# A two-layer hybrid backbone: the input gain of its linear recurrence, computed from tanh(x) and a squared decay, or from tanh(x/2) and the decay itself

## The chip, the cores and the metric

The kernel is one program on one core of a Trainium2 chip. The metric is device time in microseconds, the median of several runs. The profile and the trace come from one profiled execution. TensorE is called PE below, ScalarE is ACT, VectorE is DVE, GpSimd is POOL, and SP is the engine whose queue issues the DMAs.

## The reference, cut to what matters

The reference runs two layers over 1024 latent tokens and 256 context tokens. Each layer projects its input, runs three token mixers on the projections (global attention, windowed attention and a bidirectional gated linear recurrence), projects back, and runs a squared-ReLU MLP. The change touches the recurrence alone:

```python
def rglru_coeffs(x, w_a, b_a, w_i, b_i, lam):
    r = sigmoid(block_matmul(x, w_a) + b_a)
    i = sigmoid(block_matmul(x, w_i) + b_i)
    log_a = -LRU_C * r * softplus(-lam)
    u = sqrt(-expm1(2.0 * log_a)) * (i * x)
    return exp(log_a), u
...
h[n] = a[n] * h[n - 1] + u[n]
```

The recurrence is 512 channels wide and runs forwards and backwards over the context followed by the latent tokens. With x = log_a and a = exp(x), the factor in u is the root of 1 - a^2.

## The kernel before, in words

Features lie on the 128 partitions and tokens along the free axis. Tokens come in three tiles: two of 512 latent tokens (tile 0 and tile 1) and one of 256 context tokens (tile 2). The 512 channels of the recurrence are four chunks of 128. A product of two fp32 matrices is three matmuls on halves that are split into a high and a low part (lines 503 to 505, 685 to 687, 834 to 836 and others).

For each layer, Python generators write the work of several streams in turn: the convolution `conv_all`, the recurrence `lru_all`, the projections `side`, the attention `heads`, and in layer 0 the modulation. `weave` picks the stream that has the lowest sum of yielded costs so far, divided by a rate per stream. So the text order of the program hangs on the yielded costs alone. Within it, a scheduler decides at build time, by a simulated timeline (`schedule_with_timeline_sim=True`), in which order each engine gets its instructions. On the chip each engine then takes them in that order, one after the other.

`lru(c)` does the recurrence of one chunk c. `gates(d)` runs the gate matmuls of direction d into PSUM tiles named gate (a pool of four, shared with other work), then a Tanh for either gate, a DVE instruction for the input gate (line 693), and a third Tanh into the tile lt: t = tanh(x), since its scale and bias are both `nsp`, which is -4 softplus(-lam), and r is the tanh of half the gate's argument. `recur(d)` then runs two loops over the three token tiles:

- In the first loop ACT computes q = a^2 (the tile a2, printed as a) and a by two Exp instructions, and DVE computes (q + 1) * t at line 712, in place in lt.
- In the second loop ACT takes Ln of -t and Exp of half of that, both in place in lt. DVE multiplies u (the tile gate) by it at line 721, and runs the scan (line 724 forwards, line 729 backwards). The backward scan writes into q. Then the two directions are added (line 735) and multiplied by the gelu of the gate branch (line 736), and the result is stored by a DMA (line 737).

In the first chunks of a layer, while no attention job is prepared yet, the gates of both directions come first and the two `recur` are woven; `prog["prep"]` decides that.

Every activation goes through the helper `act` (line 131 in the profile), so the profile tells ACT's instructions apart by their tiles. Two table sets are used: Exp and Ln are in one, Tanh and Gelu in another. The helper puts a table load (line 127) where the set changes in the text order, and all instructions that need a set are kept between its load and the next one. Copies, squares and the like are in every set and may stand anywhere.

The tiles gate0, gate1, lt and a2, the tables tcos and tsin of the rotary embedding, q and k loads (qf, kf) and others share the pool `p` of 26 buffers of 128x512 fp32.

Of the kernel before, what the change touches and what calls it, by code (L numbers as in the profile page):

```python
# [11 lines left out]
AF = mybir.ActivationFunctionType  # L12
ALU = mybir.AluOpType
# [4 lines left out]
P = 128  # L18
# [3 lines left out]
DEPTH = 2  # L22
# [70 lines left out]
TOK = (512, 512, 256)  # L93
# [6 lines left out]
def tile_hybrid_backbone(ctx: ExitStack, tc: tile.TileContext, x, ctxt, cc, w_mod, b_mod, gains,  # L100
# [14 lines left out]
    vec = nc.vector  # L115
# [8 lines left out]
    def act(out, in_, func, **kw):  # L124
        want = tset.get(func)
        if want is not None and want != win["set"]:
            ld = nc.scalar.preload_act_table_set(want)
            for i in win["ins"]:
                tc.add_manual_dep(ld.ins, i.name, nosync, reason="table set")
            win.update(set=want, load=ld.ins, ins=[])  # L130
        r = nc.scalar.activation(out, in_, func, **kw)  # L131
        if want is not None:
            tc.add_manual_dep(r.ins, win["load"].name, nosync, reason="table set")
            win["ins"].append(r.ins)
        return r
# [15 lines left out]
    def weave(*pairs):  # L151
        live = [[g, rate, 0.0] for g, rate in pairs]
        while live:
            it = min(live, key=lambda v: v[2])
            try:
                cost = next(it[0])
            except StopIteration:
                live.remove(it)
                continue
            it[2] += cost / it[1]  # L160
            yield cost
# [14 lines left out]
    def utile(tt, dt=F32, name="ut"):  # L176
        if tt == CT:
            key = PAIRS.get(name, name)
            if key in halves:
                return halves.pop(key)  # L180
            t = upool.tile([P, 2, CTX], dt, tag="u", name=name + "c")
            halves[key] = t[:, 1, :]
            return t[:, 0, :]
        return upool.tile([P, 512], dt, tag="u", name=name)

    def ptile(n=512, dt=F32, name="pt"):
        return ppool.tile([P, 512], dt, tag="p", name=name)[:, 0:n]
# [7 lines left out]
    def sctile(n=512, name="sct"):  # L195
        return ps_sc.tile([P, n], F32, tag="sc", name=name)
# [4 lines left out]
    def cview(shape):  # L201
        n = int(np.prod(shape[1:]))
        v = cbuf[:, used[0]:used[0] + n]
        used[0] += n
        names = "abcde"[:len(shape) - 1]
        if len(names) > 1:
            v = v.rearrange("p (%s) -> p %s" % (" ".join(names), " ".join(names)),
                            **{m: d for m, d in zip(names, shape[1:])})
        return v
# [41 lines left out]
    c_eps, c_tiny, c_half = kc[:, 0:1], kc[:, 1:2], kc[:, 2:3]  # L251
# [13 lines left out]
    ab, th, e, z, z2, ser = (sp[:, i, :] for i in range(6))  # L265
# [19 lines left out]
    nsp = cview([P, DEPTH, 2, 4])  # L285
    vec.scalar_tensor_tensor(th, ser, 2.0, th, ALU.mult, ALU.add)
    vec.tensor_scalar(nsp.rearrange("p a b c -> p (a b c)"), th, -4.0, None, ALU.mult)
    nsp2 = cview([P, DEPTH, 2, 4])
    vec.tensor_scalar(nsp2.rearrange("p a b c -> p (a b c)"), th, -8.0, None, ALU.mult)

    def rstd_of(ps, n, bank=False, dst=None):
        l = ptile(n, name="rl")
# [294 lines left out]
    for l in range(DEPTH):  # L587
# [83 lines left out]
        def lru(c):  # L671
            dirs = ((2, 0, 1), (2, 1, 0))
            st1 = {}
            ghi, glo = gate_w[c]

            def gates(d):
                sc = nsp[:, l, d, c:c + 1]
                for tt in dirs[d]:
                    n = TOK[tt]
                    xh, xl = xs_split[c, tt]  # L680
                    res = []
                    for gi in range(2):
                        ps = sctile(n, "gate")
                        g = 2 * d + gi
                        mm(ps, ghi[:, g, :], xh, start=True, stop=False)
                        mm(ps, ghi[:, g, :], xl, start=False, stop=False)
                        mm(ps, glo[:, g, :], xh, start=False, stop=True)
                        s = ps if gi else ptile(n, name="gate0")
                        act(s, ps, AF.Tanh, scale=0.5, bias=lrubh[:, l, d, gi, c:c + 1])
                        res.append(s)  # L690
                    r, ig = res
                    i = ptile(n, name="gate1")
                    vec.scalar_tensor_tensor(i, ig, 1.0, XC[c, tt], ALU.add, ALU.mult)
                    t = ptile(n, name="lt")
                    act(t, r, AF.Tanh, scale=sc, bias=sc)
                    st1[d, tt] = (r, i, t)
                    if prog["prep"] == 0:
                        yield n / 256

            def gelus():  # L700
                for tt in outs:
                    act(GR[c, tt], GR[c, tt], AF.Gelu_apprx_tanh)

            def recur(d):
                sc, sc2 = nsp[:, l, d, c:c + 1], nsp2[:, l, d, c:c + 1]
                sq = {}
                for tt in dirs[d]:
                    a, u, t = st1[d, tt]
                    q = sq[tt] = ptile(TOK[tt], name="a2")
                    act(q, a, AF.Exp, scale=sc2, bias=sc2)  # L710
                    act(a, a, AF.Exp, scale=sc, bias=sc)
                    vec.scalar_tensor_tensor(t, q, 1.0, t, ALU.add, ALU.mult)
                    yield TOK[tt] / 400
                st = 0.0
                for tt in dirs[d]:
                    n = TOK[tt]
                    a, u, t = st1[d, tt]
                    q = sq[tt]
                    act(t, t, AF.Ln, scale=-1.0, bias=c_tiny)
                    act(t, t, AF.Exp, scale=0.5, bias=c_half)  # L720
                    vec.tensor_tensor(u, u, t, ALU.mult)
                    if d == 0:
                        h = utile(tt, name="hs")
                        vec.tensor_tensor_scan(h, a, u, st, ALU.mult, ALU.add)
                        st = h[:, n - 1:n]
                        HS[c, tt] = h
                    else:
                        h = q
                        vec.tensor_tensor_scan(h[:, ::-1], a[:, ::-1], u[:, ::-1], st, ALU.mult, ALU.add)
                        st = h[:, 0:1]  # L730
                        if tt in outs:
                            while (c, dirs[0][-1]) not in HS:
                                yield 0.5
                            hs = HS[c, tt]
                            ENG[HADD[l]].tensor_tensor(hs, hs, h, ALU.add)
                            ENG[HMUL[l]].tensor_tensor(hs, hs, GR[c, tt], ALU.mult)
                            nc.sync.dma_start(out=qd[f"f{4 + c}", tt], in_=hs)
                    yield n / 220

            pause = 1.5 if prog["prep"] == 0 else 5.0  # L740
            if cf["MERGE"] and prog["prep"] == 0:
                yield from gates(0)
                yield from gates(1)
                gelus()
                yield pause
                prog["conv"] = c + 1
                yield from weave((recur(0), 1), (recur(1), cf["MR"]))
            else:
                yield from gates(0)
                yield pause  # L750
                prog["conv"] = c + 1
                yield from recur(0)
                yield from gates(1)
                gelus()
                yield pause
                yield from recur(1)
# [629 lines left out]
```

## Time and profile before

| what | value |
| --- | --- |
| median of three runs | 3071.71 us (3069.28 to 3073.61) |
| the profiled execution | 3065.88 us |
| its span, first to last instruction | 3064.1 us |
| mean granted clock of TensorE | 0.975 |

The span is 1.8 us shorter than the profiled execution's own time, and that time is 5.8 us below the median. A granted clock of 1.00 is 2.4 GHz and one of 0.50 is 1.2 GHz; numbers between are means over a stretch. Times in the rows are in microseconds from the first instruction. The recurrence runs from about 120 to 305 us in layer 0 and from about 1790 to 1970 us in layer 1.

### The profile page before, as it was taken

Reading aid. Unit: us, or ns where it says so; the run is one execution under the profiler, and the core shown is the slowest. Engines: PE = TensorE matmul, PEld = TensorE weight load, DVE = VectorE, ACT = ScalarE, POOL = GpSimd, SP = SyncE. Lnnn points to the kernel's source line nnn. Section 1 sums busy time; section 2 is a strip of 40 time slices with the busy share of each in tenths; the row PEclk is TensorE's granted clock in tenths of the full one; section 3 lists DMA queues with packets and bytes.
Section 4 is the critical chain, followed back from the end, with each engine's and each line's share of the span. In section 5 each row is a group of like instructions: output and inputs, shape, how many; then the busy total and the mean of one; then the engine's idle time right before and its main releaser. Section 6 shows DMA issues by size and latency. Waiting matters only on the chain. (4 is left out here: it accounts for less than half of the span.)

```text
span 3064.1 us, 39201 instructions
## 1 busy us (share of the span) xinstructions
PE 2886.9 (94%) x14562; PEld 2213.2 (72%) x14562; DVE 1680.3 (55%) x2695; ACT 1225.7 (40%) x2284; POOL 1144.8 (37%) x883
## 2 busy tenths in 40 slices
PE   6997899999998999999999799699998999999997
PEld 4876645546877888888888688454466888888886
DVE  6776664556367243334736876785374562333465
ACT  4587343345343312112323578543354332112232
POOL 1453232333555322223434231343356543334232
PEclk9998999999999999999999899899998999999999
DMA  7222554434233111112213412320043321111142
GB/s 248 64 85 93 169 163 146 160 125 151 93 121 127 42 39 38 35 42 69 97 59 117 150 59 71 134 70 31 15 136 108 116 95 49 48 49 59 61 153 66
DMA packets 169424, 287.27 MB, mean 94 GB/s; under 512 B 23824, under 2 KB 37648, under 8 KB 169232
## 3 DMA queue, kind: packets, MB, share of 16 engines
q1 hardware_dynamic: 169232, 284.76, 28.5%
q8 instruction: 114, 1.87, 0.3%
q14 instruction: 78, 0.64, 0.1%
HBM read 249.56 MB, written 35.13 MB: 93 GB/s over the span
## 5 line engine op out<-in xcount | busy, mean ns | idle before, releaser
L481 POOL TENSOR_TENSOR wlo<-raw,whi 128x512 fp32r<-128x512 f32 x484 | 699.2, 1459 | 722.0 <-ACT whi L131 417.8
L1219 DVE TENSOR_TENSOR acc<-acc,m 128x512 f32<-128x512 f32 (+1 forms) x488 | 321.3, 675 | 319.7 <-PE m L1212 318.6
L1211 PE MATMUL m<-h1lo,whi 128*128 128x512 f32 (+1 forms) x1296 | 474.7, 367 | 4.4 <-DVE h1lo L1201 4.4
L1212 PE MATMUL m<-h1hi,wlo 128*128 128x512 f32 (+1 forms) x1296 | 472.3, 367 | 0.0
L131 ACT ACTIVATE whi<-raw 128x512 fp32r<-128x512 f32 x552 | 325.1, 621 | 353.7 <-PE m L1211 157.6
L1210 PE MATMUL m<-h1hi,whi 128*128 128x512 f32 (+1 forms) x1296 | 457.6, 367 | 3.1 <-ACT sq L131 1.5
L503 PE MATMUL m<-hhi,whi 128*128 128x512 f32 x1024 | 403.1, 394 | 5.2 <-ACT hhi L131 5.2
L504 PE MATMUL m<-hlo,whi 128*128 128x512 f32 x1024 | 400.4, 391 | 2.9 <-DVE hlo L519 2.9
L505 PE MATMUL m<-hhi,wlo 128*128 128x512 f32 x1024 | 399.6, 390 | 0.0
L1197 POOL TENSOR_TENSOR relu<-relu 128x512 f32<-128x512 f32 (+1 forms) x160 | 161.9, 1012 | 617.3 <-ACT relu L131 597.5
L1201 DVE TENSOR_TENSOR h1lo<-relu,h1hi 128x512 fp32r<-128x512 f32 (+1 forms) x160 | 142.7, 892 | 443.6 <-ACT h1hi L131 443.6
L131 ACT ACTIVATE relu<-m 128x512 f32<-128x512 f32 (+1 forms) x160 | 88.3, 552 | 581.5 <-PE m L505 571.8
L1211 PEld LDWEIGHTS m<-h1lo,whi 128*128 128x128 f32 x1296 | 244.6, 189 | 45.7 <-DVE h1lo L1201 5.2
L1210 PEld LDWEIGHTS m<-h1hi,whi 128*128 128x128 f32 x1296 | 242.7, 189 | 46.3 <-DVE acc L1219 2.1
L1212 PEld LDWEIGHTS m<-h1hi,wlo 128*128 128x128 f32 x1296 | 244.6, 189 | 41.3
L503 PEld LDWEIGHTS m<-hhi,whi 128*128 128x128 f32 x1024 | 193.6, 189 | 47.3 <-ACT hhi L131 6.8
L504 PEld LDWEIGHTS m<-hlo,whi 128*128 128x128 f32 x1024 | 193.1, 189 | 44.0 <-DVE hlo L519 3.6
L505 PEld LDWEIGHTS m<-hhi,wlo 128*128 128x128 f32 x1024 | 192.9, 188 | 40.8
L131 ACT ACTIVATE prob<-sc 128x512 f32<-128x512 f32 (+3 forms) x288 | 141.3, 530 | 201.9 <-PE sc L970 191.6
L995 POOL TENSOR_TENSOR prob<-prob 128x1024 f32<-128x1024 f32 (+2 forms) x62 | 134.5, 2170 | 227.2 <-ACT prob L131 138.7
L989 PE MATMUL pv<-prob,vt 128*64 128x512 f32 (+3 forms) x576 | 199.0, 552 | 2.3 <-ACT prob L131 1.6
L503 PE MATMUL zin<-hhi,whi 128*128 128x512 f32 x424 | 171.6, 405 | 1.9 <-DVE zsh L789 1.9
(344 smaller groups left out, 5289.6 us busy)
## 6 DMA issues: line engine op xcount, KB each, us to landing
raw<-in_w SPq DMA_DIRECT2D x392, 256.0 KB, 3.5
rawm<-in_w_mod SPq DMA_DIRECT2D x192, 256.0 KB, 4.2
raw<-in_w_in SPq DMA_DIRECT2D x88, 256.0 KB, 3.1
raw<-in_w_out SPq DMA_DIRECT2D x64, 256.0 KB, 4.0
xres<-xs SPq DMA_DIRECT2D x40, 256.0 KB, 5.1
xs<-y SPq DMA_DIRECT2D x32, 256.0 KB, 2.5
fc<-qf SPq DMA_DIRECT2D x30, 256.0 KB, 4.6
tcos<-in_cos SPq DMA_DIRECT2D x24, 256.0 KB, 3.3
```

The lines of the kernel that those rows point to most:

```text
L131: r = nc.scalar.activation(out, in_, func, **kw)
L481: (vec if on_dve(key) else gp).tensor_tensor(lo, raw, f(hi), ALU.subtract)
L503: mm(ps, wh, xh, start=(k == first), stop=False)
L504: mm(ps, wh, xl, start=False, stop=False)
L505: mm(ps, wl, xh, start=False, stop=(k == last))
L989: mm(pv[half[h], q0:q1], V[kt, j][:, vcol + 64 * h:vcol + 64 * h + HD], pt[:, h, :], start=(ui == 0), stop=(ui == len(units) - 1), skip_gr ...
L1197: gp.tensor_tensor(r, r, r, ALU.mult)
L1201: vec.tensor_tensor(lo, r, f(hi), ALU.subtract)
L1210: mm(ps, wh, h1[p][0][:, c0:c1], start=(p == 0), stop=False)
L1211: mm(ps, wh, h1[p][1][:, c0:c1], start=False, stop=False)
L1212: mm(ps, wl, h1[p][0][:, c0:c1], start=False, stop=(p == 1))
L1219: vec.tensor_tensor(a, a, ps, ALU.add)
```

## The change

With x = log_a, 1 - a^2 = -(1 + a^2) tanh(x), and also 1 - a^2 = -(1 + a)^2 tanh(x/2). The kernel before takes the root of the first form. The changed kernel takes (1 + a) times the root of -tanh(x/2). The scale and bias of the third Tanh are half as large. The Exp that made q is gone, and with it the tile a2. Ln and Exp of the root move from the second loop to the first, in front of the Exp that makes a. DVE still has two elementwise instructions for each tile: u times the root, now in the first loop, and (a + 1) times u, now in the second. The backward scan writes into t. The yields keep their places and costs.

```diff
-    nsp2 = cview([P, DEPTH, 2, 4])
-    vec.tensor_scalar(nsp2.rearrange("p a b c -> p (a b c)"), th, -8.0, None, ALU.mult)
+    nsph = cview([P, DEPTH, 2, 4])
+    vec.tensor_scalar(nsph.rearrange("p a b c -> p (a b c)"), th, -2.0, None, ALU.mult)
...
             def gates(d):
-                sc = nsp[:, l, d, c:c + 1]
+                sc = nsph[:, l, d, c:c + 1]
...
             def recur(d):
-                sc, sc2 = nsp[:, l, d, c:c + 1], nsp2[:, l, d, c:c + 1]
-                sq = {}
+                sc = nsp[:, l, d, c:c + 1]
                 for tt in dirs[d]:
                     a, u, t = st1[d, tt]
-                    q = sq[tt] = ptile(TOK[tt], name="a2")
-                    act(q, a, AF.Exp, scale=sc2, bias=sc2)
+                    act(t, t, AF.Ln, scale=-1.0, bias=c_tiny)
+                    act(t, t, AF.Exp, scale=0.5, bias=c_half)
                     act(a, a, AF.Exp, scale=sc, bias=sc)
-                    vec.scalar_tensor_tensor(t, q, 1.0, t, ALU.add, ALU.mult)
+                    vec.tensor_tensor(u, u, t, ALU.mult)
                     yield TOK[tt] / 400
                 st = 0.0
                 for tt in dirs[d]:
                     n = TOK[tt]
                     a, u, t = st1[d, tt]
-                    q = sq[tt]
-                    act(t, t, AF.Ln, scale=-1.0, bias=c_tiny)
-                    act(t, t, AF.Exp, scale=0.5, bias=c_half)
-                    vec.tensor_tensor(u, u, t, ALU.mult)
+                    vec.scalar_tensor_tensor(u, a, 1.0, u, ALU.add, ALU.mult)
...
-                        h = q
+                        h = t
```

## Rows read from the trace of the kernel before

**Rows 1.** The page: busy time, share of the span and instructions of each engine.

```profile
PE 2886.9 (94%) x14562; PEld 2213.2 (72%) x14562; DVE 1680.3 (55%) x2695; ACT 1225.7 (40%) x2284; POOL 1144.8 (37%) x883
```

**Rows 2.** Instructions on the tile a (ns min/median/max); engine idle until (us, times).

```profile
L131 ACT ACTIVATE a<-gate,cbuf x48: 587/803/819, 139.2 to 1949.8; 128x512 f32<-128x512 f32 x32, 128x256 f32<-128x256 f32 x16
L712 DVE SCALAR_TENSOR_TENSOR lt<-a,lt x48: 418/684/1780, 139.8 to 1953.7; 128x512 f32<-128x512 f32 x32, 128x256 f32<-128x256 f32 x16
...
  ACT a L131: 35.6, 24
```

**Rows 3.** The same view of the tile lt.

```profile
L131 ACT ACTIVATE lt<-lt,cbuf x96: 492/709/727, 141.9 to 1955.1; 128x512 f32<-128x512 f32 x64, 128x256 f32<-128x256 f32 x32
...
  ACT lt L131: 16.8, 14
```

**Rows 4.** Waits of PE from 100 to 340 us: total, times, longest.

```profile
PE gate L685 <- ACT gate L131: 8.4, 2, 7.1
PE mx L901 <- ACT qh L131: 7.4, 1, 7.4
PE mx L913 <- DVE zsh L789: 5.1, 1, 5.1
PE zin L503 <- DVE zsh L789: 1.9, 1, 1.9
```

**Rows 5.** Waits of PE from 1760 to 2070 us.

```profile
PE mx L901 <- ACT qh L131: 14.2, 1, 14.2
PE mx L913 <- DVE zsh L789: 4.2, 1, 4.2
PE vps L834 <- ACT gl L131: 3.6, 1, 3.6
PE zn L806 <- DVE cbuf L908: 3.5, 1, 3.5
```

**Rows 6.** Timeline of PE: the first matmul after the gap in layer 0.

```profile
250.34 0.79 PE L685 MATMUL gate<-xh,ghi 128*128 128x512 f32 x1 [7.07 <-ACT gate L131]
```

**Rows 7.** Timeline of ACT in the stretch before that gap ends.

```profile
235.13 0.59 ACT L131 ACTIVATE a<-gate,cbuf 128x256 f32<-128x256 f32 x1
235.62 0.49 ACT L131 ACTIVATE lt<-lt,cbuf 128x256 f32<-128x256 f32 x1
236.02 0.59 ACT L131 ACTIVATE gate<-gate,cbuf 128x256 f32<-128x256 f32 x1
...
241.39 0.80 ACT L131 ACTIVATE a<-gate,cbuf 128x512 f32<-128x512 f32 x1
242.10 1.32 ACT L131 ACTIVATE lt<-lt,cbuf 128x512 f32<-128x512 f32 x2
...
248.52 1.28 ACT L127 ACT_TABLE_LOAD   x1
```

**Rows 8.** Windows: stretch, its length, busy time by engine, granted clock, DMA share, GB/s.

```profile
233.00:250.00 17.00, 10.27 (x81) 9.66 (x79) 9.40 (x15) 16.89 (x27) 1.68 (x2) 0.90 0.00 1
250.30:253.50 3.20, 3.16 (x12) 2.87 (x13) 3.20 (x4) 3.20 (x9) 0.19 (x2) 0.51 0.12 41
...
1881.60:1885.00 3.40, 3.40 (x16) 3.40 (x17) 3.40 (x6) 2.56 (x5) 1.97 (x2) 0.50 0.23 74
...
1936.60:1976.00 39.40, 14.55 (x57) 9.51 (x55) 37.64 (x73) 20.72 (x36) 9.86 (x7) 0.71 0.30 104
```

**Rows 9.** Timeline of ACT at the end of layer 0's recurrence.

```profile
298.81 1.38 ACT L131 ACTIVATE kh<-kf 128x512 fp32r<-128x512 f32 x2 [1.82 <-DVE rl L296]
300.51 0.63 ACT L131 ACTIVATE qh<-qf 128x512 fp32r<-128x512 f32 x1 [0.32 <-DMA qf<-qb]
```

**Rows 10.** Timeline of ACT in layer 1, at two gaps of PE.

```profile
1876.38 0.63 ACT L131 ACTIVATE whi<-raw 128x512 fp32r<-128x512 f32 x1 [0.79 <-DVE a L729]
...
1880.94 0.60 ACT L131 ACTIVATE gl<-zin 128x512 f32<-128x512 f32 x1
...
1951.74 0.62 ACT L131 ACTIVATE qh<-qf 128x512 fp32r<-128x512 f32 x1
```

## The prediction

> **What bounds the kernel now.** I read the page first. PE is busy for 94% of the span and ACT for 40% [rows 1]. So an ACT instruction is worth something only where PE stands still for it, and I looked for those places. The tile view gives what the change removes; the waits of PE, asked for the stretches of the recurrence alone, give where PE stands. In layer 0 one wait of 7.1 us stands out: a gate matmul waits for an ACT gate instruction. After it come, at the end of the recurrence, 7.4 us for qh (ACT) and 5.1 us for zsh (DVE) [rows 4]. In layer 1 there is 3.6 us for gl (ACT), then 14.2 us for qh, 4.2 us for zsh and 3.5 us for a DVE reduction [rows 5]. Elsewhere in these stretches PE is fed.
>
> The gap of layer 0 is plainly ACT's. It ends at 250.34 [rows 6]. ACT was busy for 16.89 of the 17 us from 233 to 250, PE for 10.27 [rows 8], and the work is one chunk's `recur`, then a table load at 248.52 [rows 7]. The gate matmuls of the next chunk had filled their PSUM tiles, and the Tanh that empties them may only run behind that load. After the gap PE runs 3.2 us at a granted clock of 0.51 [rows 8], that is, at 1.2 GHz after having stood still.
>
> **The change, part by part.**
>
> *The removed Exp.* There are 48, 32 of 512 columns and 16 of 256 [rows 2]; two layers of four chunks make eight, so a chunk has four and two. ACT starts the next instruction a little before the one before it ends, so I price them by the distance of starts: 242.10 - 241.39 = 0.71 us for 512 columns, and 235.62 - 235.13 = 0.49 us for 256 [rows 7]. A chunk saves 4 x 0.71 + 2 x 0.49 = 3.8 us of ACT time, the kernel eight times that, 30 us. What counts is where PE waits for it:
>
> - The gap of layer 0 (7.07 us): all six stand in front of the Tanh, and ACT has no idle time into which the saving could go. It shrinks by 3.8 us, to 3.3. The clock may add to that: the 3.2 us at half speed did the work of 1.6. The 3.6 us gap of layer 1 was followed by 3.4 us at 0.50 as well [rows 8], so a gap of 3.3 us may still cost the clock. I take 0 and keep 1.6 as an end.
> - The end of layer 0: qh there starts 0.32 us after idle time that a DMA ended, and kh waited for DVE before it [rows 9]. ACT is not saturated; the chain runs through DVE, the store of a projection and its reload. It gets shorter only as far as DVE waited for ACT before. Ends are 0 and 3.8; I take 1, nearer to the end without gain, since the row names DMA.
> - The 3.6 us gap of layer 1: gl starts at 1880.94 behind a run of the recurrence. But ACT idled 0.79 us for DVE at 1876.38 [rows 10], so part of the saving would fall into that wait. Ends 0 and 3.6; I take 2, about the middle.
> - The end of layer 1: qh starts at 1951.74 [rows 10] and ends the 14.2 us wait; the six removed Exp of the last chunk all stand before it. But from 1936.6 to 1976 DVE is busy for 37.64 of 39.4 us [rows 8], and the later waits of PE there are for DVE. A qh 3.8 us earlier meets a full DVE queue, whose work stays. DVE's idle time, 39.4 - 37.64 = 1.8 us, is what can be gained without another order; I take 1.5, and 3.8 as the far end.
>
> *The moved Ln and Exp.* No instruction is added: 96 before and after [rows 3]. Moved in front of the Exp for a, they no longer wait for a DVE result that itself waited for ACT. That round trip cost DVE 35.6 us of idle time at line 712 [rows 2] and 16.8 us at line 721 [rows 3]. DVE is not the bound in most of these stretches, so I book nothing for it. The price is that the first DVE instruction of a tile now waits for Ln and Exp where it waited for one Exp: this is the second rival below. No DMA is moved, and no queue of SP or POOL is passed by anything but shorter waits.
>
> *The DVE instructions.* Two elementwise ones for each tile before and after, all operands in SBUF, so 0. Their spread is wide: line 712 takes 418 to 1780 ns, 684 in the median [rows 2], and the slow ones lie beside POOL work. Whether the moved ones land beside POOL more often I can't see; an extra 1.1 us each (1780 - 684) on DVE is the bound, against the same gained where they escape it. By the Trainium skill, page "SBUF — State Buffer", section "SBUF: two separate sides", DVE instructions with two SBUF inputs and GpSimd instructions that read SBUF exclude one another for a whole instruction. Taken alone that rule would allow any of the moved ones to turn slow, where the row's median says that most are not.
>
> *The tile a2.* It leaves the pool of 26 buffers, six at a time in the woven chunks. Less waiting for buffers can only start loads earlier; the PE waits above name other causes, so 0, with the gain inside the ends already given.
>
> *The set-up and table loads.* One constant instead of another, and the set changes in the text order at the same places: 0.
>
> The sum is 3.8 + 1 + 2 + 1.5 = 8.3 us. The profiled execution took 3065.88 us, so it would take 3057.6; its time lies 5.8 us below the median of the runs, and on that median I get 3071.7 - 8.3 = 3063.4 us, 0.27% less. About 0.2%, 6 us, is what a measurement of this kernel can tell from no change.
>
> The largest gain of all terms is 3.8 + 1.6 in the first gap, 3.8 at the end of layer 0, 3.6 + 1.7 (half of 3.4 us of slow clock) in the third, 3.8 at the last: 18.3 us. With a few microseconds for slow clock behind the two end gaps, about 3050 us.
>
> **The rivals.**
>
> *1. The gain is given back; no change.* PE's own work is untouched, 2886.9 us [rows 1]. The 3.8 us won at 250 us can be lost at 301 us if kh and qh come when the DMA brings them, and in layer 1 DVE sets the end at 1976 whatever ACT does. For it speak DVE's 37.64 of 39.4 us and the DMA in front of qh [rows 8, 9]. Against it speaks that what ends late there also started late: the last chunk's gates come after the gap, so that chain moves forward with it. Time: 3071.7 us, or 3067.9 if the first gap alone counts. The planner that orders the queues may also fill the free time of ACT with other work in front of the Tanh, so that the change does nothing there. By the Trainium skill, page "Perfetto Trace Analysis", section "Identifying Performance Opportunities", a kernel gets better mainly through its most-contended engine. That is PE here, and the rule would leave the time as it is; the same page also says to look at the gaps of that engine, and the 7.07 us gap is one that ACT ends [rows 6].
>
> *2. DVE waits longer in the first loop; slower.* In that loop a tile of 512 columns now takes ACT Ln, Exp and Exp, where it took two Exp. Ln or Exp on lt costs 1.32 - 0.71 = 0.61 us by the distance of starts, and 0.40 for 256 columns (236.02 - 235.62) [rows 7]. So the loop takes 2 x 0.61 - 0.71 = 0.51 us more for 512 columns and 2 x 0.40 - 0.49 = 0.31 for 256, and a chunk's last product comes 4 x 0.51 + 2 x 0.31 = 2.7 us later. DVE works in order: if zsh, kl and the reductions for the attention stand behind it, PE gets them 2.7 us later. PE waited for DVE in four places: zsh twice in layer 0 and zsh and the reduction in layer 1 [rows 4, 5]. Four times 2.7 is 10.8 us, less the 3.8 of the first gap: 7.0 slower, 3078.7 us. It decides only if at least three of the four are queued that way. Against it: the second loop then has no wait for ACT at all, so the same queue catches up within the chunk.
>
> **How the numbers follow.** The forecast, faster by more than 0.2%, gets 0.54: with 3.8 us from the first gap it needs 2.4 us more, and I book 4.5 in the other three places. Rival 1, within 0.2%, gets 0.29, and rival 2, slower by more than 0.2%, gets 0.17. The range from 3050 to 3077 us leaves about 0.05 out below and up to 0.15 above, the larger part of rival 2. The forecast's own range is 3050 to 3065.
>
> **What would show it.** Right: 48 fewer ACT instructions and some 34 us less ACT time (32 x 0.80 + 16 x 0.60); no Exp into the tile a; the wait of the gate matmul near 245 us down from 7.1 to about 3.3; the waits for gl and for qh in layer 1 each shorter by 1 to 4 us; DVE no longer idle for a tile a. Wrong: the first gap as long as it was, for instance because other ACT work moved in front of the Tanh; or the first gap shorter and the waits for qh, zsh and the reductions longer by as much; or longer DVE idle time for lt in the first loop with PE waiting behind it. If gaps move outside these two stretches, the order of the queues has changed, and my terms are not what decides.

## The result and the profile after

The changed kernel takes 3110.6 us (median, 3106.0 to 3123.7) against 3070.5 us for the kernel before in the same runs: a ratio of 1.0138, interval 1.0105 to 1.0172. It is 40 us slower; the prediction was 3063.4 us, with a range from 3050 to 3077.

The line of the page that answers to [rows 1], of the kernel after:

```profile
PE 2924.6 (94%) x14562; PEld 2236.6 (72%) x14562; DVE 1651.2 (53%) x2695; ACT 1209.2 (39%) x2236; POOL 1126.3 (36%) x883
```

ACT lost its 48 instructions and 16.5 us. PE ran the same 14562 matmuls and was busy for 37.7 us longer. The profiled spans are 3064.1 and 3104.1 us, so of 40.0 us more, 37.7 are PE's work and 2.3 its idle time.

Where these 37.7 us lie is seen in the view of stretches, one row for each stage: set-up with the recurrence of layer 0, its attention with the projection back, MLP and projections, recurrence of layer 1, its attention, its MLP. The columns are the stretch, its length, busy time (and instructions) of PE, PEld, DVE, ACT and POOL, granted clock, DMA share and GB/s. First the kernel before:

```profile
0.00:300.00 300.00, 251.76 (x1422) 208.50 (x1422) 204.13 (x359) 206.33 (x364) 106.82 (x88) 0.96 0.37 122
300.00:810.00 510.00, 480.36 (x2767) 287.51 (x2768) 285.09 (x518) 203.22 (x417) 186.68 (x144) 0.97 0.46 149
810.00:1780.00 970.00, 940.97 (x4869) 804.14 (x4868) 499.30 (x776) 303.55 (x578) 357.38 (x289) 0.99 0.24 77
1780.00:1935.00 155.00, 151.31 (x815) 131.27 (x814) 104.88 (x153) 129.66 (x224) 47.10 (x35) 0.99 0.23 76
1935.00:2390.00 455.00, 405.49 (x1780) 241.13 (x1779) 271.10 (x440) 195.38 (x362) 195.33 (x142) 0.94 0.24 78
2390.00:3064.10 674.10, 657.06 (x2917) 540.60 (x2915) 315.81 (x450) 187.53 (x341) 251.48 (x189) 0.99 0.24 78
```

The same view of the kernel after, with the stages cut where nearly the same work ends (see the counts of matmuls):

```profile
0.00:300.00 300.00, 248.44 (x1422) 206.93 (x1422) 199.77 (x358) 188.22 (x337) 110.59 (x89) 0.97 0.36 118
300.00:830.00 530.00, 497.93 (x2754) 296.55 (x2755) 281.76 (x518) 205.85 (x416) 176.84 (x141) 0.94 0.44 143
830.00:1800.00 970.00, 943.91 (x4875) 805.49 (x4874) 492.78 (x777) 308.92 (x578) 351.11 (x291) 0.99 0.24 78
1800.00:1960.00 160.00, 152.36 (x812) 130.90 (x811) 101.42 (x153) 117.14 (x205) 48.02 (x34) 0.98 0.22 72
1960.00:2430.00 470.00, 425.07 (x1782) 254.51 (x1781) 265.26 (x440) 194.59 (x358) 192.89 (x142) 0.93 0.23 76
2430.00:3104.00 674.00, 656.91 (x2926) 542.20 (x2924) 310.16 (x451) 194.47 (x344) 246.87 (x192) 0.99 0.24 79
```

The two attention stages got 20 and 15 us longer, and in them PE is busy for 17.6 and 19.6 us more with nearly the same matmuls (13 fewer and 2 more). The change touches not a line of the attention. The MLPs are within 3 us of what they were, and the recurrence of layer 1 is 5 us longer.

Which matmuls these are is told by the same view of one tile over the whole run (stretch, length, busy time of PE, PEld and the engine that reads the tile; the end at 3130 lies behind the span). The first row is the scores sc, the second the maxima mx; the kernel before:

```profile
0.00:3130.00 3130.00, 203.30 (x1152) 129.37 (x1152) 141.31 (x288) 0.97 0.28 92
0.00:3130.00 3130.00, 89.12 (x352) 44.60 (x352) 170.09 (x336) 0.97 0.28 92
```

The kernel after:

```profile
0.00:3130.00 3130.00, 225.17 (x1152) 144.47 (x1152) 143.97 (x288) 0.97 0.28 92
0.00:3130.00 3130.00, 101.88 (x352) 52.06 (x352) 171.73 (x336) 0.97 0.28 92
```

So the 1504 matmuls of sc and mx cover 34.6 us more of PE's time (21.9 and 12.8). They contract over 64 rows: head 0 in one half of the array, head 1 in the other. The timeline of PE shows what is different (start, duration, line, tiles, how many). In the kernel before, the two heads stand next to each other:

```profile
450.14 0.40 PE L970 MATMUL sc<-qh,kh 64*128 64x512 f32 x2
450.37 0.40 PE L970 MATMUL sc<-ql,kh 64*128 64x512 f32 x2
450.60 0.39 PE L970 MATMUL sc<-qh,kl 64*128 64x512 f32 x2
450.83 0.39 PE L970 MATMUL sc<-qm,neg_sb 64*128 64x512 f32 x2
451.06 0.39 PE L921 MATMUL mx<-kh,qh 64*128 64x512 f32 x1
```

In the kernel after there are places where one head stands alone:

```profile
457.58 0.40 PE L966 MATMUL sc<-qh,kh 64*128 64x512 f32 x1
457.59 0.50 PE L917 MATMUL mx<-kh,qh 64*128 64x512 f32 x1
457.82 0.39 PE L966 MATMUL sc<-ql,kh 64*128 64x512 f32 x1
458.06 0.39 PE L966 MATMUL sc<-qh,kl 64*128 64x512 f32 x1
458.29 0.39 PE L966 MATMUL sc<-qm,neg_sb 64*128 64x512 f32 x1
```

From 450.14 to 451.06 PE does eight matmuls of 512 columns, two at a time, each pair in 0.23 us. From 457.82 to 458.29 the steps are 0.23 and 0.24 us as well, but each holds one matmul. In these rows the second of a pair costs nothing, and alone it costs 0.23 us. The Trainium skill, page "TensorEngine Tiling (Array Packing)", section "Theoretical Speedup", gives up to 2x where the contraction is over 64 rows at most; these rows agree. Over the whole kernel a pair gains less: in the kernel before, a pair of sc with 512 columns covers 0.29 us on average and a single one 0.22, so a pair saves 0.15 us.

**How far the pairs go.** I went through PE's queue in the two programs and paired off neighbours of different halves, each matmul in one pair at most. In the kernel before 806 of the 1504 matmuls are in such pairs, in the kernel after 646. That is 80 pairs fewer, at up to 0.23 us each 18 us at most, and 12 at the average of 0.15. A second part is the clock. I summed PE's busy time over the stretches in which the trace has a granted clock of 0.50: 85.7 us before, 115.1 after. At 0.50 a matmul takes about twice as long (in the kernel after the gate matmuls of 512 columns start 0.43 us apart at 0.50, at 246.38 and 246.81 us, and 0.23 us apart at 1.00, at 260.87 and 261.10), so PE's busy time less half of that is its **work at full clock**: 2886.9 - 42.8 = 2844.1 us before, 2924.6 - 57.5 = 2867.1 after. So 23.0 of the 37.7 us are work in the same matmuls, and 14.7 come from work done at 1.2 GHz. All of the 23.0 lies in sc and mx: counted as the time by which their matmuls move PE's end on, and corrected for the clock in the same way, sc takes 177.7 us before and 189.8 after, mx 59.8 and 70.9. The lost pairs explain 12 to 18 us of it; where the rest comes from is not shown.

**Why the queue changed.** The planner of this kernel first lays the work out with the numbers of buffers that are written in the kernel. For the kernel before it finds no order that way, and raises five numbers by one. It says so when the program is built:

```
the starting buffer counts deadlocked; feasible after 1 bump round(s); {'p_p_64': '26→27',
'mm_ps_mm_76': '3→4', 'raw_raw_70': '6→7', 'hi_wsp_73': '6→7', 'sc_ps_sc_79': '4→5'}
```

For the kernel after, without a2 in the pool p, the written numbers do, and they stay: 3 for mm and 4 for sc, both PSUM. The scores take their tiles from sc. The maxima mx take head 0's from sc and head 1's from mm, which the projections use too. So the theory: **the change took away two PSUM buffers that nobody had written down, and with them the pairs.** The rivals: the recurrence itself (ACT's or DVE's new order) costs the time; or the order changed in other ways, and the pairs are only a part.

### The profile page after: what moved, and what is told of

It reads as the page before. It is cut to its first block, busy times and chain, and to the rows that moved or that the text cites. A ratio compares the mean times of both kernels' runs of the same rounds, so it can differ in the third digit from the quotient of the medians.

```text
span 3104.1 us, 39454 instructions
## 1 busy us (share of the span) xinstructions
PE 2924.6 (94%) x14562; PEld 2236.6 (72%) x14562; DVE 1651.2 (53%) x2695; ACT 1209.2 (39%) x2236; POOL 1126.3 (36%) x883
## 4 chain that ended last, share of the span: by engine, by line
PE 77%; DVE 9%; ACT 3%; issue 3%; DMA 2%; POOL 1%; SPq 0%; POOLq 0%; DVEq 0%; ACTq 0%
PE m L504 8%; PE m L503 8%; PE m L505 8%; PE m L1206 8%; PE m L1207 8%; PE m L1208 8%; PE sc L966 6%; PE pv L985 5%; PE yps L503 2%; PE yps L504 2%; PE yps L505 2%; PE zin L503 2%; PE zin L504 2%; DVE sq L322 2%; PE zin L505 2%
## 5 line engine op out<-in xcount | busy, mean ns | idle before, releaser
L481 POOL TENSOR_TENSOR wlo<-raw,whi 128x512 fp32r<-128x512 f32 x484 | 671.9, 1402 | 1118.3 <-ACT whi L131 946.6
L131 ACT ACTIVATE whi<-raw 128x512 fp32r<-128x512 f32 x552 | 333.4, 626 | 716.0 <-PE m L1207 363.3
L1197 DVE TENSOR_TENSOR h1lo<-relu,h1hi 128x512 fp32r<-128x512 f32 (+1 forms) x160 | 118.0, 737 | 345.0 <-ACT h1hi L131 344.3
L1208 PEld LDWEIGHTS m<-h1hi,wlo 128*128 128x128 f32 x1296 | 243.9, 188 | 40.1 <-POOL wlo L481 0.5
```

The source lines that it names most:

```text
L481: (vec if on_dve(key) else gp).tensor_tensor(lo, raw, f(hi), ALU.subtract)
L1208: mm(ps, wl, h1[p][0][:, c0:c1], start=False, stop=(p == 1))
```

## The experiments

Expectations and results count for sc and mx the time by which their matmuls move PE's end on, each overlap once: in the kernel before 179.7 and 63.8 us, after 194.7 and 77.8. "Side by side" is the count of above. Idle is span less PE's busy time. Each ratio is to the kernel before in the same session, where it took 3070.5 to 3071.2 us. The last four columns are of the one profiled execution, which can lie off the median: 9.7 us below it in after with 4, 5 and written pairs, 8.0 below in before in the places of after, 5.2 above in after with 4 and 5. Executions of one kernel differ with their mean granted clock: the twelve of after with 4 and 5 go from 3060.5 us at 0.975 to 3077.9 us at 0.968.

| kernel | us, median | ratio to before, interval | side by side | PE busy | at 0.50 | work at full clock | idle |
| --- | --- | --- | --- | --- | --- | --- | --- |
| before | 3070.5 | 1 | 806 | 2886.9 | 85.7 | 2844.1 | 177.2 |
| after | 3110.6 | 1.0138 (1.0105 to 1.0172) | 646 | 2924.6 | 115.1 | 2867.1 | 179.5 |
| after, mm 4, sc 5 | 3066.0 | 0.9983 (0.9972 to 0.9994) | 806 | 2896.8 | 110.9 | 2841.4 | 172.6 |
| before, p 27 | 3114.8 | 1.0135 (1.0118 to 1.0151) | 634 | 2934.7 | 137.0 | 2866.2 | 178.3 |
| before, p 27, mm 4, sc 5 | 3062.2 | 0.9968 (0.9955 to 0.9981) | 788 | 2891.3 | 95.2 | 2843.7 | 167.0 |
| after, mm 4 | 3068.0 | 0.9991 (0.9980 to 1.0001) | 740 | 2897.0 | 115.6 | 2839.2 | 169.9 |
| after, sc 5 | 3103.9 | 1.0113 (1.0096 to 1.0130) | 748 | 2908.2 | 116.3 | 2850.0 | 191.7 |
| after, pairs written | 3086.4 | 1.0052 (1.0037 to 1.0067) | 1232 | 2894.7 | 129.0 | 2830.2 | 187.7 |
| after, mm 4, sc 5, pairs written | 3057.7 | 0.9958 (0.9942 to 0.9973) | 1310 | 2866.4 | 88.8 | 2822.0 | 179.8 |
| before, p 27, mm 4, sc 5, pairs written | 3044.0 | 0.9904 (0.9886 to 0.9923) | 1316 | 2873.4 | 108.7 | 2819.1 | 170.9 |
| after in the places of before, mm 4, sc 5 | 3060.9 | 0.9963 (0.9949 to 0.9978) | 804 | 2889.8 | 91.4 | 2844.1 | 170.1 |
| before in the places of after, p 27, mm 4, sc 5 | 3052.0 | 0.9937 (0.9917 to 0.9958) | 806 | 2885.0 | 84.2 | 2842.9 | 157.2 |
| after, mm 5, sc 6, pairs written | 3032.7 | 0.9870 (0.9855 to 0.9885) | 1364 | 2847.6 | 105.0 | 2795.1 | 182.7 |

**After, with the numbers that before was given.**

```diff
-    ps_mm = ctx.enter_context(tc.tile_pool(name="ps_mm", bufs=3, space=PSUM))
-    ps_sc = ctx.enter_context(tc.tile_pool(name="ps_sc", bufs=4, space=PSUM))
+    ps_mm = ctx.enter_context(tc.tile_pool(name="ps_mm", bufs=4, space=PSUM))
+    ps_sc = ctx.enter_context(tc.tile_pool(name="ps_sc", bufs=5, space=PSUM))
```

> The kernel after, with 4 buffers for the tiles mm in place of 3 and 5 for the tiles sc in place of 4 (the numbers that the planner gives the kernel before). Theory: the change freed the buffers of a2, the planner therefore left these two numbers at 3 and 4, and with them the two heads' matmuls of 64 rows stand side by side less often in PE's queue; with the numbers of before the arithmetic of after gives 3056 to 3068 us, PE's busy time falls from 2924.6 to about 2885, sc from 194.7 to about 180 and mx from 77.8 to about 64 us. Rival A, the recurrence itself costs the time (ACT's or DVE's new order of work): stays at 3100 to 3115 us with PE's busy time at about 2925. Rival B, the rest of the order changed and the pairs are only a part: about 3080.

3066.0 us: the whole loss is gone, with the arithmetic of after untouched. The page, and the rows of sc and mx over the whole run:

```profile
PE 2896.8 (94%) x14562; PEld 2218.1 (72%) x14562; DVE 1639.2 (53%) x2695; ACT 1202.1 (39%) x2236; POOL 1122.3 (37%) x883
...
0.00:3130.00 3130.00, 205.29 (x1152) 130.06 (x1152) 140.82 (x288) 0.97 0.28 92
0.00:3130.00 3130.00, 91.22 (x352) 45.53 (x352) 169.98 (x336) 0.97 0.28 92
```

sc and mx are within 2.1 us of the kernel before, and work at full clock is back: 2841.4 us. PE's busy time came to 2896.8 where I wrote 2885; the difference is time at 0.50, which stayed at 110.9 us. Rival A is out, and so is the 3080 us of rival B; but the two numbers change the whole order of the queues, so this run alone does not say how much of the gain is the pairs.

**Before, with one buffer more in p.** The other way round: the arithmetic of before, and a number with which the planner raises none.

```diff
-    ppool = ctx.enter_context(tc.tile_pool(name="p", bufs=26))
+    ppool = ctx.enter_context(tc.tile_pool(name="p", bufs=27))
```

> The kernel before, its arithmetic untouched, with 27 buffers for the tiles of pool p written down in place of 26 (the planner then finds an order at once and leaves mm at 3 and sc at 4). Theory: the arithmetic is not what costs; 3095 to 3115 us, PE busy about 2925, sc about 195, mx about 78. Rival A: 3070 us, as before, since the recurrence is that of before. Rival B: about 3085.

3114.8 us. One more SBUF buffer, and the kernel before loses 44 us and takes as long as the kernel after. Its page and its rows of sc and mx:

```profile
PE 2934.7 (94%) x14562; PEld 2239.5 (72%) x14562; DVE 1660.8 (53%) x2695; ACT 1228.4 (39%) x2284; POOL 1135.3 (36%) x883
...
0.00:3130.00 3130.00, 223.86 (x1152) 143.43 (x1152) 143.54 (x288) 0.97 0.28 92
0.00:3130.00 3130.00, 101.18 (x352) 51.52 (x352) 172.13 (x336) 0.97 0.28 92
```

They are those of the kernel after within 1.4 us, and the work at full clock too (2866.2 against 2867.1). PE's busy time is 10 us above the 2925 that I wrote, with 137.0 us of it at 0.50.

**Before, with 27, 4 and 5 written down**, all three edits above together.

> The kernel before with 27, 4 and 5 buffers for p, mm and sc written down: the partner of the run of after with 4 and 5, so that the two differ in the arithmetic alone. Theory: 3065 to 3077 us, and 4 to 10 us above the kernel after with the same numbers (the 8.3 us that the prediction gave the arithmetic). Rival A: 3070 us and at least 30 below the kernel after with the same numbers.

3062.2 us. So it is not the number 27 that costs; the two PSUM numbers decide with either arithmetic, and the other two numbers that the planner had raised (raw and hi) are not needed for it. The second half of my expectation failed: this kernel is not 4 to 10 us slower than the kernel after with the same numbers but 3.8 us faster, which the two intervals do not tell from none.

**A second profile of after with 4 and 5.**

> A second profile of the kernel after with 4 and 5 buffers for mm and sc: every theory expects the same gaps of PE as in the first, within 0.3 us a gap, and the same PE busy time within 1 us; it shows how far a gap of one profiled execution can be trusted.

PE was busy for 2894.9 us against 2896.8, a little more than I allowed, and its work at full clock is 2841.3 us against 2841.4. Gaps repeat less well: one at 204 us took 4.64 and 3.87 us, one at 387 us 1.82 and 2.97. A single gap of one profile is good to about 1 us, not 0.3.

**One number at a time**, each of the two lines of the first diff by itself.

> The kernel after with 4 buffers for mm in place of 3, sc left at 4. If each number sets its own tiles' place in PE's queue: mx falls from 77.8 to about 64 us of PE's time, sc stays near 195, and the time lies about half way between after (3110) and after with both numbers (3066): 3085 to 3100 us. If one of the two numbers decides alone: 3066 or 3110.

> The kernel after with 5 buffers for sc in place of 4, mm left at 3. If each number sets its own tiles' place: sc falls from 194.7 to about 180 us, mx stays near 77, 3085 to 3100 us. If one of the two decides alone: 3066 or 3110.

With mm alone 3068.0 us, with sc alone 3103.9. That is the second case of what I wrote, one number that decides alone: mm is worth nearly all. With mm 4, mx takes 68.9 us and sc falls as well, to 184.3. With sc 5, work at full clock falls by 17 us to 2850.0, but idle time rises by 12 to 191.7: fewer lone matmuls, and PE waits in their place. The count of pairs does not tell these two kernels apart: 740 stand side by side with mm 4 and 748 with sc 5, while the times lie 36 us apart. So the numbers do more than set the pairs. That mm counts so much fits that head 1's maxima share it with the projections, but no run shows that step by itself.

**The pairs by themselves.** The numbers stay at 3 and 4, and the order of the two heads is written down for the planner, with no wait on the chip:

```diff
-                        mm(ps[h], st, q[half[h], q0:q1], start=(pi == 0), stop=(pi == 3))
+                        m = mm(ps[h], st, q[half[h], q0:q1], start=(pi == 0), stop=(pi == 3))
+                        if last is not None:
+                            tc.add_manual_dep(m.ins, last.name, nosync, reason="side by side")
+                        last = m.ins
```

> The kernel after with mm and sc left at 3 and 4, and an order of the two heads' matmuls sc written down: head 0, head 1, head 0, head 1, with no wait added on the chip. If the pairs are what the time went for: a pair of 128x512 took 0.294 us (60.9 us over 207 in the kernel before) and a single one 0.221 (78.2 over 354), so a pair saves 0.15 us; sc falls from 194.7 to about 165 us and the time from 3110 by 20 to 35 us, to 3075 to 3090. If the buffers are what PE lacks, and the lost pairs are only their mark: PE's gaps grow by what sc loses, 3100 to 3120 us.

3086.4 us, 24 less, in the range for the pairs: sc takes 161.7 us. But idle time grows by 8.2 us to 187.7, and mx, which has no written order, stays at 73.2. So written pairs give back a little more than half of the loss. But 1232 matmuls stand side by side here, far more than the 806 of the kernel before, so the 24 us are not the worth of the 80 lost pairs: they show that pairs are worth time, and that the numbers of buffers act by more than the pairs.

Both together, the written pairs and the numbers 4 and 5:

> The kernel after with 4 and 5 buffers for mm and sc, and the same written order of the matmuls sc. If PE's own time is the bound in the attention: sc falls from 180.5 to about 162 us, 3066 becomes 3045 to 3055 us, below both kernels. If pairs in front of each other wait for PSUM and ACT: 3060 to 3085 us, with more gaps of PE in the attention.

3057.7 us, between the two expectations: sc fell to 155.3 us, and idle time rose by 7.2.

**The parts of the change, with the queue in order.** In one kernel after's Ln, Exp and multiplication go back to the second loop; in the other Ln and Exp of before go to the first.

```diff
-                    act(t, t, AF.Ln, scale=-1.0, bias=c_tiny)
-                    act(t, t, AF.Exp, scale=0.5, bias=c_half)
                     act(a, a, AF.Exp, scale=sc, bias=sc)
-                    vec.tensor_tensor(u, u, t, ALU.mult)
+                    vec.scalar_tensor_tensor(u, a, 1.0, u, ALU.add, ALU.mult)
...
-                    vec.scalar_tensor_tensor(u, a, 1.0, u, ALU.add, ALU.mult)
+                    act(t, t, AF.Ln, scale=-1.0, bias=c_tiny)
+                    act(t, t, AF.Exp, scale=0.5, bias=c_half)
+                    vec.tensor_tensor(u, u, t, ALU.mult)
```

And the second, in recur of the kernel before:

```diff
                     vec.scalar_tensor_tensor(t, q, 1.0, t, ALU.add, ALU.mult)
+                    act(t, t, AF.Ln, scale=-1.0, bias=c_tiny)
+                    act(t, t, AF.Exp, scale=0.5, bias=c_half)
...
-                    act(t, t, AF.Ln, scale=-1.0, bias=c_tiny)
-                    act(t, t, AF.Exp, scale=0.5, bias=c_half)
```

> The kernel after with 4 and 5 buffers for mm and sc, and with Ln, the Exp of the root and the multiplication by u back in the second loop: the arithmetic of after in the places of before. It removes the Exp of the square and moves nothing. If the removed Exp alone shortens PE's first gap of the recurrence of layer 0 (7.07 us in before, 5.56 and 2.09 in before with 27, 4 and 5, none over 0.4 us in after with 4 and 5), the gap stays under 1 us here; if the move of Ln and Exp is what matters, it is 4 us or more. The time: 3055 to 3075 us, whichever, since the rest of the order is worth as much as this gap.

> The kernel before with 27, 4 and 5 buffers for p, mm and sc, and with Ln and the Exp of the root moved to the first loop: the arithmetic of before in the places of after. ACT has four instructions a tile ahead of a yield in place of two, and removes none. If ACT's work ahead of the next gates sets PE's first gap, the gap grows from 5.56 and 2.09 to 9 us or more, and the gap of 10.12 and 2.92 us at the end of layer 0 shrinks by 1 to 3; if the order that the planner finds sets it, the gap stays between 0 and 8 us without a direction. The time: 3058 to 3078 us.

3060.9 us, as expected, and 3052.0, below the expected 3058 to 3078. In the first kernel PE has no gap over 0.4 us from 225 us to the end of the recurrence, as expected if the removed Exp pays (it has one of 3.98 us that ends at 203, where after with 4 and 5 has its 4.64). The second should then have had 9 us or more. Its waits of PE from 100 to 340 us (total, times, longest):

```profile
PE mx L901 <- ACT qh L131: 8.5, 1, 8.5
PE mx L913 <- DVE zsh L789: 4.5, 1, 4.5
PE vps L834 <- ACT vt L131: 3.3, 1, 3.3
...
PE gate L685 <- ACT gate L131: 1.1, 1, 1.1
```

The 1.1 us for a gate lie at 215 us and are an earlier gap, which the same kernel without the move has as well (1.09 at 218). Where the first gap of 5.56 and 2.09 us was, PE now waits once, 3.33 us at 238.6, and for ACT's vt. With more ACT work in the first loop than any other kernel, the gap is thus shorter, within the 0 to 8 us that I wrote for the planner's order: the amount of ACT work in front of it alone does not set it. At the end of layer 0 the sum is 8.48 + 4.54 = 13.0 us, as without the move (10.12 + 2.92); I had expected 1 to 3 less.

**The best queue.** The written pairs once more, in before with 27, 4 and 5, and in after with these numbers:

```diff
-    ps_mm = ctx.enter_context(tc.tile_pool(name="ps_mm", bufs=3, space=PSUM))
-    ps_sc = ctx.enter_context(tc.tile_pool(name="ps_sc", bufs=4, space=PSUM))
+    ps_mm = ctx.enter_context(tc.tile_pool(name="ps_mm", bufs=5, space=PSUM))
+    ps_sc = ctx.enter_context(tc.tile_pool(name="ps_sc", bufs=6, space=PSUM))
```

> The kernel before with 27, 4 and 5 buffers for p, mm and sc and the order of the two heads' matmuls sc written down. If the pairs and the arithmetic are independent of each other: 8 us below the same kernel without the pairs (3062.2, as 3066.0 became 3057.7 in after), 3050 to 3058 us, sc near 157 us of PE's time; if the arithmetic of after is worth its predicted 8.3 us once the queue is the same in both: 3063 to 3068.

> The kernel after with 5 and 6 buffers for mm and sc and the written order of the matmuls sc. If the number of buffers still holds PE's queue back: mx falls from 68.7 to about 63 us and the time from 3057.7 to 3045 to 3053 us; if 4 and 5 were enough: 3052 to 3065 us, as with 4 and 5.

3044.0 us, below both expectations, and 3032.7, below them too. The second is after with 5 and 6 buffers and the written pairs, and beats both kernels: 1.3% below before. Two numbers and the written order differ from after at once here, and no run has 5 and 6 alone. Its page, and its rows of sc and mx:

```profile
PE 2847.6 (94%) x14562; PEld 2196.8 (72%) x14562; DVE 1634.6 (54%) x2695; ACT 1196.7 (39%) x2236; POOL 1123.0 (37%) x883
...
0.00:3130.00 3130.00, 169.79 (x1152) 106.48 (x1152) 135.93 (x288) 0.97 0.28 92
0.00:3130.00 3130.00, 81.59 (x352) 43.20 (x352) 168.38 (x336) 0.97 0.28 92
```

sc covers 33.5 us less than in the kernel before and mx 7.5; mx moves PE's end on by 63.5 us, near the 63 expected. PE's work at full clock is 49.0 us less with the same 14562 matmuls.

## Why the prediction was wrong, point by point

**The step that failed** is the one on a2: that the tile leaves the pool, that "less waiting for buffers can only start loads earlier", and hence 0. With it fell a sentence of rival 1, "PE's own work is untouched, 2886.9 us". I took PE's order as given and priced what the change does to its waits. But what p has to hold decided whether the planner raises five numbers or none; one buffer more in p was enough to turn it. That is worth 44.6 us in after (3110.6 to 3066.0) and 52.6 in before (3114.8 to 3062.2), five and six times my sum of 8.3. That the numbers of buffers cost the 40 us is shown both ways; that they do it through the pairs is shown in part. None of my rivals held it; the slower one was DVE in the first loop. Only the prediction's last sentence came true: gaps and work moved outside the two stretches, and my terms did not decide.

**The first gap** was to shrink by 3.8 us to 3.3. The rows of after, PE's timeline:

```profile
241.38 0.28 PE L832 MATMUL vps<-whi,hlo 128*128 128x256 f32 x1
245.79 0.80 PE L685 MATMUL gate<-xh,ghi 128*128 128x512 f32 x1 [4.12 <-ACT gate L131]
```

It is 4.12 us after 7.07 [rows 6], 2.95 less. ACT's timeline shows where the rest went:

```profile
241.68 1.28 ACT L127 ACT_TABLE_LOAD   x1
242.98 0.45 ACT L131 ACTIVATE gate<-gate,cbuf 128x256 f32<-128x256 f32 x1
243.35 1.44 ACT L131 ACTIVATE gl<-gl 128x256 f32<-128x256 f32 x3
244.70 1.04 ACT L131 ACTIVATE gate<-gate,cbuf 128x512 f32<-128x512 f32 x2
```

The load now starts as PE stops, where it came 5.25 us later before (PE stopped at 250.34 - 7.07 = 243.27, the load came at 248.52 [rows 6, 7]). Then three Gelu, 1.44 us, stand between the first Tanh and those of 512 columns. The size was near, the reason is not shown: in the eight kernels with the new arithmetic this gap was 4.12 us or less, in four of the five with the old one 7.1 to 10.2 us in all, and in the fifth, which moves Ln and Exp, it was 3.3 us and for another tile. And PE's other waits ahead of the end of layer 0 grew, as the next rows show.

**The end of layer 0** (I took 1 us off). Waits of PE from 100 to 340 us in the kernel after, which answer to [rows 4]:

```profile
PE mx L897 <- ACT qh L131: 11.3, 1, 11.3
PE gate L685 <- ACT gate L131: 6.8, 2, 4.1
PE mx L917 <- ACT qhc L131: 4.1, 1, 4.1
PE zn L802 <- ACT gate L131: 2.7, 1, 2.7
PE mx L897 <- DVE zsh L785: 2.6, 1, 2.6
PE zin L503 <- ACT gl L131: 1.9, 1, 1.9
PE gate L685 <- DVE xcc L640: 1.6, 1, 1.6
```

qh and zsh are 11.3 + 2.6 = 13.9 us where they were 12.5, and a wait for qhc is new: nothing gained, as rival 1 had it. The waits ahead of the end are 6.8 + 2.7 + 1.9 + 1.6 = 13.0 us (gate, zn, zin and gate again), where they were 8.4 + 1.9 [rows 4] and 0.9 for a DVE gate instruction, 11.2 us: the 2.95 us of the first gap were given back before qh.

**Layer 1** (I took 2 and 1.5 us off). Waits of PE from 1780 to 2090 us in the kernel after, where its recurrence now lies; they answer to [rows 5]:

```profile
PE mx L897 <- ACT qh L131: 12.3, 1, 12.3
PE mx L897 <- DVE zsh L785: 7.7, 2, 4.3
PE mx L909 <- DVE cbuf L904: 3.9, 1, 3.9
PE gate L685 <- ACT gl L131: 2.5, 1, 2.5
PE gate L685 <- DVE xcc L640: 2.2, 1, 2.2
```

The wait for gl went from 3.6 to 2.5 us (another matmul waits for it now), qh from 14.2 to 12.3: smaller, as I wrote, and then zsh from 4.2 to 7.7. What is won at qh is lost at zsh.

**ACT and DVE.** ACT lost 48 instructions but 16.5 us, not 34; between the two kernels with 4 and 5 it is 1226.6 - 1202.1 = 24.5 us. The 34 counted whole durations of instructions that overlap, where the distance of starts had given 30; and 32 x 0.80 + 16 x 0.60 is 35.2, not 34. Of rival 2, DVE did get idle for lt, 40.1 us in place of 16.8 [rows 3], while the 35.6 for a [rows 2] are gone: less in sum. With 4 and 5 written down DVE still sits idle for lt for 35.1 us, and the 40 us of loss are gone, so rival 2 is not their cause.

**The clock** behind the first gap: PE ran the next matmuls at 0.50 for the 2.8 us from 245.7 us, where it had been 3.2 us at 0.51 [rows 8], so that taking 0 there was near. That PE would work 29 us more at 0.50, most of it in the attention of layer 0, was in no term.

**What stays open.** With the numbers written down, the new arithmetic is 3.8 us slower than the old (3066.0 and 3062.2), and with the pairs written 13.7 slower; in the places of before it is 1.3 us faster, in the places of after 14.0 slower (3.8 and 1.3 are within the intervals); moving Ln and Exp gives 10.3 less with the old arithmetic and 5.1 more with the new. These signs do not agree, each kernel has its own order, and a term of 8 us cannot be told from that; no run shows the 8.3 us. Nor do the runs say why time at 0.50 lies between 84 and 137 us: it does not go with the pairs (110.9 us in after with 4 and 5, whose pairs are back). After with mm 4 alone has as much of it as after (115.6 and 115.1 us) and is 42.6 us faster.

## What to carry to other kernels

Where a planner chooses orders and buffer counts, a change that frees or takes a buffer can turn its decisions far away: look at what it decided before and after, and write down the numbers that matter, before any instruction is priced. Compare PE's busy time at equal matmul count, corrected for the granted clock, as the first thing: here it showed 23 us of new work in a kernel that had no new matmul. And matmuls over 64 rows are worth an order of their own: writing it down took 24.2, 8.3 and 18.2 us off in three kernels.

## What was not expected of the hardware

- Two matmuls of 64 rows and 512 columns in the two halves of the array took 0.23 us together and 0.23 us alone where they ran without a wait (0.29 and 0.22 on average for sc in the kernel before), and the neighbour need not be of the same product: at 457.58 and 457.59 us an sc and an mx start side by side.
- PE's work at full clock repeats to 0.1 us between two profiles of one kernel (2841.4 and 2841.3), while its busy time differs by 1.9 and single gaps by up to 1.2 us.
- The granted clock of the attention of layer 0 was 0.97 before and 0.94 after; time at 0.50 cost after 14.7 us that no count of instructions shows.
